# Token rows normed before they are turned, groups loaded one ahead, three bank pairs, recurrence over 17 slots, last projection in 3+3+2 tiles

## The chip, the cores and the metric

One core of one Trainium2 chip. The engines are TensorE (PE, with its weight loads as PEld), VectorE (DVE), ScalarE (ACT), GpSimd (POOL) and SyncE (SP), whose queue issues the DMA transfers here. The metric is the device time of one execution in microseconds (us), the median of several runs.

## What is computed

Two layers over 1040 tokens (16 meta tokens ahead of 1024) of width 1024, float32 throughout; the meta tokens are dropped at the end.

```python
h = concat(meta, x)
# layer 0: pooling mixer
v, gate = split(rmsnorm(h, w0) @ w_in)            # 1024 -> 2 x 2048
u = (trailing mean over 2, 4, 8, 16 tokens) - v   # one window per group of 512 columns
u = einsum(u, w_grp) * scale                      # per group, 512 x 512
h = h + (u * silu(gate)) @ w_out
# layer 1: HGRN2 mixer, 16 heads of 128
q, fp, i, gate = split(rmsnorm(h, w1) @ w_in)     # 1024 -> 4 x 2048
f = lb + (1 - lb) * sigmoid(fp);  k = 1 - f;  q = silu(q)
# per head, chunkwise: S_t = diag(f_t) S_{t-1} + k_t i_t^T ;  o_t = S_t^T q_t
o = rmsnorm(o, per head) * o_norm
h = h + (o * silu(gate)) @ w_out
out = rmsnorm(h[16:], final_w)
```

## The kernel before

**Products.** Activations lie turned: columns of the model on the partitions, tokens along the free dimension, in two passes of 520 tokens, each of 2 x 260 (`CH`). A float32 matmul is made of three: every operand is split into a rounded part and a rest (`split`: a cast on ScalarE, a subtraction on VectorE). The products with `pool_w_in` and `hgrn_w_in` go by a Strassen-like scheme (`products`): two column tiles at a time (v and gate; q and gate; f and i) take seven pieces P1, P2, P6, P5, P7, P3, P4 of 12 matmuls per pass. Two PSUM bank pairs take the sums: P1, P6, P7 and P4 go on in one, P2, P5 and P3 in the other, and in between ScalarE copies them out or VectorE adds them to a copy, so a piece waits for the reader of the piece before it in its pair. The split weights of a piece are made `LOOK = 3` pieces ahead.

**Order.** After each piece `tick()` runs what `later(k, fn)` put there, k pieces on, and then prepares weights. So the other work of a stage is interleaved with the pieces of the next. The framework then orders the instructions of each engine at compile time: a list schedule in which the order of emission is the priority, so a ready instruction of lower priority may stand earlier. On the chip each engine works in that order.

**Stages.** `prologue(p)`: loads five token tiles, turns each (eight transposes by PE, copied out of PSUM), and makes the norm's factor from the rows (Square, `rstd_into` on VectorE and POOL, `rbcast` as matmul L151 to spread it over the partitions); `make_T` then norms the turned halves (L270) and splits all operands of the pieces, in steps s1 to s6. Pass 1's steps run in the ticks of the first tile's pass 0. `v_gate`, `pooled`: 16 column tiles; `u` and the gate go to DRAM. `grp_stage(p)`: per group four `u` tiles are loaded and split and four column tiles multiplied (24 matmuls each, lines 499 to 501). `out_stage(p)`: eight column tiles of 96 matmuls; the residual is loaded in turned form and added on VectorE (L515). `between(p)`: turns the result back to token rows for the norm's factor and for `h_dram`, then `make_T`. Pass 0's steps run in the ticks of `grp_stage(1)`, those of pass 1 in the ticks of head 0's first product.

`mixer1`: 16 heads, each of two products (q and gate, f and i) over both passes. `scan(n)` puts the pieces of head n's recurrence into the ticks of head n+1 (`PIECES`, slots 0 to 12): `run` (a scan and four reciprocals on VectorE, L693), `turn_v`, `scale`, `score`, two levels, `turn_k`, `states`, `outs` (the sums stay in PSUM until they are normed), `gated`. Small sums and transposes use four single banks (`ps_at`).

`out1`: the last projection in four rounds of two token tiles; for each head 12 matmuls of 512 columns (lines 920 to 922). `prep` loads head n's output and gate, multiplies them (L892) and splits them; the last heads' pieces run in the ticks of round 0, what is left by `flush`. After head 15 the residual, the norm and the store follow for both tiles.

Of the kernel before, what the change touches and what calls it, by code (L numbers as in the profile page):

```python
# [40 lines left out]
PIECES = {"run": 0, "turn_v": 1, "scale": 2, "score": 4, "l32": 5, "l64": 6, "turn_k": 7, "states": 8, "outs": 10, "gated": 12}  # L41
# [7 lines left out]
def kernel(  # L49
# [22 lines left out]
    ps_mm = ctx.enter_context(tc.tile_pool(name="ps_mm", bufs=2, space=bass.MemoryType.PSUM))  # L72
    ps_at = ctx.enter_context(tc.tile_pool(name="ps_at", bufs=4, space=bass.MemoryType.PSUM))
# [6 lines left out]
    x_dram = dr.tile([KD, P, L], F32, tag="x", name="x_dram")  # L80
# [68 lines left out]
    def rbcast(dst, rstd, tn):  # L149

        pe.matmul(dst, lhsT=rstd[:tn, 0:1].to_broadcast([tn, P]), rhs=ident[:tn, :tn], start=True, stop=True)  # L151

# [4 lines left out]
    def whole(fast):  # L157
# [8 lines left out]
        def half(name):  # L166
            return un.tile([P, 2, CH], F32, tag="h", name=name, bufs=6)
# [35 lines left out]
        def wslot():  # L203
            return wp.tile([P, 2, 512], F32R, tag="w", name="w", bufs=6)
# [56 lines left out]

        def make_T(p, src, R, w):

            hn, d = [None] * 4, {}

            def norm(i):
                t = unit("hn").rearrange("p (k t) -> p k t", k=2)
                for j in range(2):
                    k = 2 * i + j
                    vec.scalar_tensor_tensor(t[:, j], src[i][:, j], w[:, k : k + 1], R, mul, mul)  # L270
                hn[i] = t.rearrange("p k (c t) -> p k c t", c=2)
# [8 lines left out]
            def B(k, c):  # L280
                return [hn[2 * k + i][:, :, c] for i in range(2)]
# [10 lines left out]
            def s1():  # L292
                norm(0), norm(1)
                put("P1", B(0, 0))

            def s2():
                norm(2), norm(3)
                put("P2", B(1, 0))
# [18 lines left out]
            return [s1, s2, s3, s4, s5, s6]  # L317

# [47 lines left out]

        def token_stats(xt, tn, R, t0):

            ssq, r = small("ssq"), small("rstd", 6)
            act.activation(xt[:tn, :D], xt[:tn, :D], AF.Square, accum_out=ssq[:tn, 0:1])  # L370
            rstd_into(r, ssq, tn, 1, D)
            rb = atbank()
            rbcast(rb[:, :tn], r, tn)
            vec.tensor_copy(R[:, t0 : t0 + tn], rb[:, :tn])

        def load_tokens(p):
            out_ = []
            for t0, tn in TP[p]:
                xt = unit("xt")
                if t0 == 0:  # L380
                    nc.sync.dma_start(xt[:tn, :D], meta_tokens)
                else:
                    nc.sync.dma_start(xt[:tn, :D], x[t0 - META : t0 - META + tn])
                out_.append(xt)
            return out_

        def prologue(p):

            xr = [unit("xr").rearrange("p (k t) -> p k t", k=2) for _ in range(4)]
            R = half("R").rearrange("p a b -> p (a b)")  # L390
            toks = load_tokens(p)

            def turn(i):
                (t0, tn), xt = TP[p][i], toks[i]
                o = t0 - p * PT
                for h in range(2):
                    b = atbank().rearrange("p (k t) -> p k t", t=P)
                    for k in range(4):
                        kk = h * 4 + k
                        pe.transpose(out=b[:, k, :tn], in_=xt[:tn, kk * P : (kk + 1) * P], identity=ident[:tn, :tn])  # L400
                    act.copy(xr[2 * h][:, :, o : o + tn], b[:, 0:2, :tn])
                    vec.tensor_copy(xr[2 * h + 1][:, :, o : o + tn], b[:, 2:4, :tn])
                token_stats(xt, tn, R, o)

            def keep():
                for i in range(4):
                    nc.sync.dma_start(
                        x_dram[2 * i : 2 * i + 2, :, p * PT : (p + 1) * PT].rearrange("k p t -> p k t"), xr[i]
                    )

            steps = make_T(p, xr, R, nw[0])
            return [lambda i=i: turn(i) for i in range(len(TP[p]))] + steps[:2] + [keep] + steps[2:]
# [55 lines left out]

        def grp_stage(p):
            a = {}  # L470
            for g in range(4):
                us, sgs = [], []
                for k in range(4):
                    ur = half("ur").rearrange("p a b -> p (a b)")
                    nc.sync.dma_start(ur, u_dram[g * 4 + k][:, p * PT : (p + 1) * PT])
                    u = unit("u", F32R).rearrange("p (h t) -> p h t", h=2)
                    split(u[:, 0], u[:, 1], ur)
                    us.append(u)
                for j in range(4):
# [9 lines left out]
                    a[m] = at  # L489
                    tick()  # L490
# [12 lines left out]
        def out_stage(p, a):  # L503
            hs = []
            for m in range(KD):
                if m % 2 == 0:
                    h = unit("h").rearrange("p (k t) -> p k t", k=2)
                    nc.sync.dma_start(h, x_dram[m : m + 2, :, p * PT : (p + 1) * PT].rearrange("k p t -> p k t"))
                    hs.append(h)
# [4 lines left out]
                o = hs[-1][:, m % 2].rearrange("p (c t) -> p c t", c=2)  # L514
                vec.tensor_tensor(o, o, ps[:, :, :CH], add)  # L515
            return hs
# [25 lines left out]
        def between(p, hs):  # L542

            R = half("R").rearrange("p a b -> p (a b)")

            def stats(t0, tn):
                ssq, r = small("ssq"), small("rstd", 6)
                ht = unit("ht")
                o = t0 - p * PT
                for h in range(2):  # L550
                    b = atbank()
                    for k in range(4):
                        kk = h * 4 + k
                        pe.transpose(
                            out=b[:tn, k * P : (k + 1) * P], in_=hs[kk // 2][:, kk % 2, o : o + tn], identity=ident
                        )
                    act.copy(ht[:tn, h * 512 : h * 512 + 512], b[:tn])
                    act.activation(b[:tn], b[:tn], AF.Square, accum_out=ssq[:tn, h : h + 1])
                if t0 > 0:
                    nc.sync.dma_start(h_dram[t0 - META : t0 - META + tn], ht[:tn, :D])  # L560
                vec.tensor_tensor(ssq[:tn, 2:3], ssq[:tn, 0:1], ssq[:tn, 1:2], add)
                rstd_into(r, ssq[:, 2:3], tn, 1, D)
                rb = atbank()
# [401 lines left out]
        for fn in prologue(0):  # L965
            fn()
# [57 lines left out]
```

## Time and profile before

| | us |
|---|---|
| median of 3 runs | 1861.88 (1861.18 to 1862.97) |
| profiled execution | 1864.24, its span 1862.5 |
| PE busy | 1718.2 (92%) |
| PEld busy | 1648.1 (88%) |
| VectorE busy | 1256.9 (67%) |
| ScalarE busy | 756.9 (41%) |
[...]

The span runs from the first to the last instruction; 1.74 us of the execution lie around it. Busy shares are means over stages with different limits, and since matmuls are pipelined, busy PE is not PE at its peak.

### The profile page before, as it was taken

Reading aid. Unit: us, or ns where it says so; the run is one execution under the profiler, and the core shown is the slowest. Engines: PE = TensorE matmul, PEld = TensorE weight load, DVE = VectorE, ACT = ScalarE, POOL = GpSimd, SP = SyncE. Lnnn points to the kernel's source line nnn. Section 1 sums busy time; section 2 is a strip of 40 time slices with the busy share of each in tenths; the row PEclk is TensorE's granted clock in tenths of the full one; section 3 lists DMA queues with packets and bytes.
Section 4 is the critical chain, followed back from the end, with each engine's and each line's share of the span. In section 5 each row is a group of like instructions: output and inputs, shape, how many; then the busy total and the mean of one; then the engine's idle time right before and its main releaser. Section 6 shows DMA issues by size and latency. Waiting matters only on the chain.

```text
span 1862.5 us, 32892 instructions
## 1 busy us (share of the span) xinstructions
PE 1718.2 (92%) x13531; PEld 1648.1 (88%) x13531; DVE 1256.9 (67%) x2018; ACT 756.9 (41%) x1696; POOL 49.4 (3%) x70
## 2 busy tenths in 40 slices
PE   4699999998997799699999999999999999988997
PEld 3599999988997699599999999999999999977885
DVE  5766767876425833787778777778877778875432
ACT  4443333344225422535544445444445544444221
POOL 1100000000000000000000000000000000000000
PEclk9899999998998799799999999999999999999999
DMA  4333332356425442211212112112212112245542
GB/s 128 119 109 103 108 111 92 112 177 218 151 91 182 141 127 70 85 58 53 67 47 69 52 57 63 58 58 58 66 50 63 53 58 58 80 158 176 171 142 69
DMA packets 202078, 181.90 MB, mean 98 GB/s; under 512 B 8030, under 2 KB 176046, under 8 KB 201918
## 3 DMA queue, kind: packets, MB, share of 16 engines
q1 hardware_dynamic: 201918, 179.71, 30.6%
q8 instruction: 108, 1.77, 0.4%
q14 instruction: 52, 0.43, 0.1%
HBM read 133.08 MB, written 46.60 MB: 96 GB/s over the span
## 4 chain that ended last, share of the span: by engine, by line
PE 75%; DVE 12%; ACT 6%; issue 4%; POOL 2%; DMA 1%; SPq 0%; DVEq 0%; ACTq 0%; POOLq 0%
PE mm L338 14%; PE mm L340 13%; PE mm L339 13%; PE mm L500 5%; PE mm L499 5%; PE mm L501 5%; DVE F L693 4%; PE at L662 2%; POOL rstd L104 2%; PE at L920 2%; PE at L922 2%; PE at L921 2%; PE at L708 2%; PE at L807 2%; ACT on L834 2%
## 5 line engine op out<-in xcount | busy, mean ns | idle before, releaser
L338 PE MATMUL mm<-Th,w 128*128 128x260 f32 x2688 | 782.3, 291 | 43.2 <-DVE Q L611 23.3
L339 PE MATMUL mm<-Tl,w 128*128 128x260 f32 x2688 | 768.1, 286 | 5.4 <-DVE Tl L147 5.3
L340 PE MATMUL mm<-Th,w 128*128 128x260 f32 x2688 | 768.3, 286 | 0.0
L338 PEld LDWEIGHTS mm<-Th,w 128*128 128x128 f32 x2688 | 513.5, 191 | 52.4 <-DVE Q L611 26.4
L339 PEld LDWEIGHTS mm<-Tl,w 128*128 128x128 f32 x2688 | 513.7, 191 | 8.0 <-DVE Tl L147 7.9
L340 PEld LDWEIGHTS mm<-Th,w 128*128 128x128 f32 x2688 | 513.7, 191 | 0.7
L146 ACT CAST w<-raw 128x512 fp32r<-128x512 f32 x346 | 207.0, 622 | 256.0 <-PE mm L501 193.5
L147 DVE TENSOR_TENSOR w<-raw,w 128x512 fp32r<-128x512 f32 x346 | 232.0, 685 | 117.0 <-ACT w L146 116.4
L344 ACT COPY P<-mm 128x520 f32<-128x520 f32 (+1 forms) x150 | 85.8, 572 | 185.9 <-PE mm L340 185.6
L499 PE MATMUL mm<-a,w 128*128 128x260 f32 x512 | 145.2, 284 | 0.0
L500 PE MATMUL mm<-a,w 128*128 128x260 f32 x512 | 144.3, 282 | 0.0
L501 PE MATMUL mm<-a,w 128*128 128x260 f32 x512 | 143.8, 281 | 0.0
L693 DVE RECIPROCAL F<-X 128x260 f32<-128x260 f32 x64 | 106.9, 1733 | 0.0
L147 DVE TENSOR_TENSOR w<-S,w 128x512 fp32r<-128x512 f32 x100 | 67.5, 686 | 57.1 <-ACT w L146 57.1
L499 PE MATMUL mm<-u,w 128*128 128x260 f32 x256 | 78.4, 311 | 25.2 <-ACT u L146 25.2
L501 PEld LDWEIGHTS mm<-a,w 128*128 128x128 f32 x512 | 96.3, 188 | 0.0
L500 PEld LDWEIGHTS mm<-a,w 128*128 128x128 f32 x512 | 96.3, 188 | 0.0
L499 PEld LDWEIGHTS mm<-a,w 128*128 128x128 f32 x512 | 96.1, 188 | 0.0
L104 POOL TENSOR_TENSOR rstd<-rstd,nhalf 128x1 f32<-128x1 f32 (+4 forms) x44 | 43.3, 984 | 1789.8 <-DVE rstd L103 1150.4
L500 PE MATMUL mm<-u,w 128*128 128x260 f32 x256 | 78.3, 307 | 2.9 <-DVE u L147 2.8
L146 ACT CAST w<-S 128x512 fp32r<-128x512 f32 x100 | 60.9, 627 | 42.7 <-DVE S L236 36.4
L499 PEld LDWEIGHTS mm<-u,w 128*128 128x128 f32 x256 | 53.7, 212 | 26.7 <-ACT u L146 26.4
(160 smaller groups left out, 2605.6 us busy)
## 6 DMA issues: line engine op xcount, KB each, us to landing
raw<-in_hgrn_w_in_dram SPq DMA_DIRECT2D x66, 512.0 KB, 4.2
raw<-in_pool_w_in_dram SPq DMA_DIRECT2D x34, 512.0 KB, 5.3
raw<-in_pool_w_out_dram SPq DMA_DIRECT2D x32, 512.0 KB, 3.6
u_dram<-d SPq DMA_DIRECT2D x16, 520.0 KB, 2.7
ur<-u_dram SPq DMA_DIRECT2D x32, 260.0 KB, 3.7
sgh<-s_dram SPq DMA_DIRECT2D x32, 260.0 KB, 3.7
raw<-in_pool_w_grp_dram SPq DMA_DIRECT2D x16, 512.0 KB, 3.6
a_dram<-og SPq DMA_DIRECT2D x16, 512.0 KB, 2.7
```

The source lines that it names most:

```text
L104: pool.tensor_tensor(r[:tn, :n], r[:tn, :n], nhalf[:tn, :n], ALU.pow)
L146: act.copy(hi, src)
L147: vec.tensor_tensor(lo, src, hi.bitcast(F32), sub)
L338: pe.matmul(o, lhsT=w[:, 0, ks], rhs=th[:, k], start=first, stop=False, **kw)
L339: pe.matmul(o, lhsT=w[:, 0, ks], rhs=tl[:, k], start=False, stop=False, **kw)
L340: pe.matmul(o, lhsT=w[:, 1, ks], rhs=th[:, k], start=False, stop=k == 3, **kw)
L344: act.copy(t[:, s], bs)
L499: pe.matmul(o, lhsT=w[:, 0, ks], rhs=xs[k][:, 0, cs], start=first and k == 0, stop=False)
L500: pe.matmul(o, lhsT=w[:, 0, ks], rhs=xs[k][:, 1, cs], start=False, stop=False)
L501: pe.matmul(o, lhsT=w[:, 1, ks], rhs=xs[k][:, 0, cs], start=False, stop=last and k == 3)
L662: pe.matmul(b[s0 : s0 + h, c * h : (c + 1) * h], lhsT=K0[:, c * P + s0 : c * P + s0 + h], rhs=Q[:, c * P + s0 + h : c * P + s0 + 2 * h], s ...
L693: vec.reciprocal(iX[:, s], X[:, s])
```

## The change

- `tokens(p, w, ys)` takes the place of `prologue` and `between`: per tile, `first` loads the rows of x, adds the result of the layer (turned to rows, VectorE), stores them in `h_dram`, and norms the rows (Square, `rstd_into`, a scaled copy on ScalarE); `second`, two steps later, turns the normed rows and multiplies by the norm's weights on the way out of PSUM. `x_dram`, `rbcast` and the norm in `make_T` go. Before the second layer's pass 0 the steps run in every second tick.
- `group(p, g)` loads and splits the `u` tiles of a group one group ahead; the first of each pass in the stage before.
- `ps_mm` has three pairs in place of two, `ps_at` two banks in place of four; `half` tiles 8 in place of 6, `wslot` 5 in place of 6.
- Head 0's two products run in pass 0 first and then in pass 1.
- The recurrence has 17 slots: the reciprocals and the scores stand alone, `outs` copies its sums out of PSUM, `normed` follows, and `gated` multiplies by the gate (loaded as `gl`), which `prep` did.
- `out1` has rounds of 3, 3 and 2 token tiles; the last three heads of a round are multiplied tile by tile, each tile's end behind its own.

```diff
+PIECES = {
+    "run": 0, "turn_v": 1, "inv0": 1, "inv1": 2, "scale_q": 2, "inv2": 3, "inv3": 4, "scale_k": 5, "scale_e": 6,
+    "score0": 6, "score1": 7, "to32": 8, "l32": 9, "l64": 10, "turn_k": 11, "states": 12, "outs": 14, "normed": 16, "gated": 17,
+}
...
+        def tokens(p, w, ys=None):
+            hn, held = [], {}
+            def first(i):
+                t0, tn = TP[p][i]
+                o = t0 - p * PT
+                ht, sq = unit("ht"), unit("sq")
+                src = meta_tokens if t0 == 0 else x[t0 - META : t0 - META + tn]
+                nc.sync.dma_start(ht[:tn, :D], src)
+                ssq, r = small("ssq", 3), small("rstd", 3)
+                if ys is not None:
...
+                        vec.tensor_tensor(hh, hh, b[:tn], add)
+                    if t0 > 0:
+                        nc.sync.dma_start(h_dram[t0 - META : t0 - META + tn], ht[:tn, :D])
+                act.activation(sq[:tn, :D], ht[:tn, :D], AF.Square, accum_out=ssq[:tn, 0:1])
+                rstd_into(r, ssq, tn, 1, D)
+                act.activation(sq[:tn, :D], ht[:tn, :D], AF.Copy, scale=r[:tn, 0:1])
+                held[i] = sq
+            def second(i):
...
+                    for k in (0, 1):
+                        kk = h * 4 + k
+                        act.activation(hn[2 * h][:, k, o : o + tn], b[:, k, :tn], AF.Copy, scale=w[:, kk : kk + 1])
+                    ww = w[:, h * 4 + 2 : h * 4 + 4].unsqueeze(2).to_broadcast([P, 2, tn])
+                    vec.tensor_tensor(hn[2 * h + 1][:, :, o : o + tn], b[:, 2:4, :tn], ww, mul)
...
+        def group(p, g):
+            us = []
+            for k in range(4):
+                ur = half("ur").rearrange("p a b -> p (a b)")
+                nc.sync.dma_start(ur, u_dram[g * 4 + k][:, p * PT : (p + 1) * PT])
+                u = unit("u", F32R).rearrange("p (h t) -> p h t", h=2)
+                split(u[:, 0], u[:, 1], ur)
+                us.append(u)
+            ready_u[p, g] = us
...
+                    if j == 0 and g < 3:
+                        group(p, g + 1)
...
+                if m == 5 and p == 0:
+                    group(1, 0)
...
-                vec.tensor_tensor(o, o, ps[:, :, :CH], add)
+                act.copy(hs[-1][:, m % 2].rearrange("p (c t) -> p c t", c=2), ps[:, :, :CH])
...
+                    act.copy(ends, X.rearrange("p (b i) -> p b i", i=16)[:, :, 15:16])
+                def inv(i):
+                    s = slice(i * CH, (i + 1) * CH)
+                    vec.reciprocal(iX[:, s], X[:, s])
...
+                    tl["g"] = [half("gl").rearrange("p a b -> p (a b)")[:, :512] for _ in range(2)]
+                    for i, g in enumerate(tl["g"]):
+                        nc.sync.dma_start(g, g_dram[n][:, META + i * 512 : META + i * 512 + 512])
...
+                        act.copy(on[b0 // 4], b)
...
-                        act.activation(og[:, b0 * P : b0 * P + 512], b, AF.Copy, scale=onorm[:, n : n + 1])
+                        vec.scalar_tensor_tensor(og[:, s], b, onorm[:, n : n + 1], tl["g"][b0 // 4], mul, mul)
...
+            puts = [[consumer(part, 0, st) for part in parts] for parts in ("qg", "fi")]
+            for p in range(2):
+                for put in puts:
+                    products((p,), *put)
+                if p == 0:
+                    flush()
...
+            ROUNDS = ((0, 3), (3, 3), (6, 2))
...
-                vec.tensor_tensor(ar, ar, gr, mul)
...
+                for n in range(HEADS - 3):
+                    fetch(r * HEADS + n + 3)
...
+                fetch((r + 1) * HEADS + 2)
+                late = [ready.pop((r, n)) for n in range(HEADS - 3, HEADS)]
...
+                    for j, w in enumerate(late):
+                        proj(ps, w, HEADS - 3 + j, i)
...
-        early(1, 2 * HEADS, lambda t: head_views(t // 2)[t % 2])
+        early(2, 2 * HEADS, view1)
...
+            if t == ME - 1:
+                later(3, lambda: group(0, 0))
...
-        spread(between(0, hs))
+        spread(tokens(0, nw[1], hs), 2)
```

## Rows read from the trace of the kernel before

**Rows 1.** Busy time of each engine by stage; last: granted clock, DMA share, GB/s.

```profile
core 0: us, PE busy (x) PEld busy (x) DVE busy (x) ACT busy (x) POOL busy (x), PEclk, DMA share, GB/s
0.00:36.02 36.02, 12.66 (x54) 10.15 (x54) 14.45 (x41) 13.74 (x29) 4.74 (x27) 1.00 0.55 163
36.02:101.40 65.38, 43.98 (x219) 39.29 (x219) 52.91 (x94) 31.38 (x59) 7.58 (x9) 0.84 0.28 95
101.40:404.63 303.23, 303.23 (x2522) 302.96 (x2520) 217.53 (x327) 107.17 (x220) 0.00 (x0) 1.00 0.34 111
404.63:469.97 65.34, 54.26 (x385) 52.63 (x385) 46.66 (x69) 28.78 (x50) 0.00 (x0) 0.87 0.69 224
469.97:561.97 92.00, 92.00 (x770) 92.00 (x769) 30.45 (x45) 22.58 (x37) 0.00 (x0) 1.00 0.38 118
561.97:647.54 85.57, 61.55 (x437) 59.09 (x436) 59.81 (x100) 43.31 (x83) 3.17 (x5) 0.82 0.51 164
647.54:739.31 91.77, 91.77 (x770) 91.77 (x769) 32.62 (x47) 20.52 (x33) 0.00 (x0) 1.00 0.33 99
739.31:811.91 72.60, 55.32 (x388) 51.42 (x387) 51.45 (x95) 38.99 (x82) 3.16 (x5) 0.84 0.26 81
811.91:1643.55 831.64, 807.09 (x7097) 790.27 (x7095) 642.93 (x991) 389.74 (x960) 24.56 (x15) 1.00 0.20 60
1643.55:1717.37 73.82, 63.15 (x330) 50.58 (x331) 51.60 (x79) 33.20 (x71) 1.64 (x1) 0.93 0.52 172
1717.37:1850.60 133.23, 133.23 (x577) 107.99 (x575) 51.86 (x126) 26.05 (x69) 3.45 (x6) 1.00 0.44 137
1850.60:1862.50 11.90, 0.00 (x1) 0.00 (x0) 4.65 (x10) 1.43 (x6) 1.10 (x2) 0.64 0.25 93
```

**Rows 2.** Waits of PE: us in total, times, longest.

```profile
PE at L151 <- POOL rstd L104: 34.1, 18, 4.2
...
PE mm L499 <- ACT u L146: 25.2, 6, 11.0
...
PE mm L338 <- DVE Q L611: 23.3, 15, 1.7
```

**Rows 3.** Timeline in head 2: VectorE's reciprocals, the add, PE's next product.

```profile
870.73 6.68 DVE L693 RECIPROCAL F<-X 128x260 f32<-128x260 f32 x4
...
877.33 0.64 DVE L611 TENSOR_TENSOR Q<-P,mm 128x520 f32<-128x520 f32 x1
...
878.02 0.39 PE L338 MATMUL mm<-Th,w 128*128 128x260 f32 x1 [1.65 <-DVE Q L611]
```

**Rows 4.** Busy time in the first column tile of `grp_stage(0)`.

```profile
408.21:414.11 5.90, 5.15 (x24) 4.85 (x25) 4.63 (x8) 1.74 (x3) 0.00 (x0) 0.56 0.95 309
```

**Rows 5.** Groups of instructions by line: busy us, mean ns.

```profile
L147 DVE TENSOR_TENSOR w<-raw,w 128x512 fp32r<-128x512 f32 x346 | 232.0, 685 | 117.0 <-ACT w L146 116.4
...
L834 ACT ACTIVATE on<-at,rstd 128x128 f32<-128x128 f32 x128 | 34.8, 383 | 32.8 <-POOL rstd L104 32.8
...
L554 PE MATMUL at<-ident,h 128*128 128x128 f32 (+3 forms) x80 | 12.4, 300 | 0.0
...
L270 DVE SCALAR_TENSOR_TENSOR hn<-xr,vecs,R 128x520 f32<-128x520 f32 x16 | 11.2, 753 | 0.0
...
L370 ACT ACTIVATE xt<-xt 128x1024 f32<-128x1024 f32 (+3 forms) x10 | 10.6, 1059 | 5.3 <-PE at L400 5.3
...
L402 DVE COPY xr<-at 128x256 f32<-128x256 f32 (+3 forms) x20 | 7.3, 373 | 6.6 <-ACT xr L401 6.6
...
L934 DVE TENSOR_TENSOR hres<-hres,at 128x512 f32<-128x512 f32 x8 | 5.2, 683 | 13.8 <-PE at L922 13.7
```

**Rows 6.** Timeline of the projection: after `outs` of head 15, its first matmul, the end.

```profile
1693.89 0.48 PE L920 MATMUL mm<-woh,w 128*128 128x512 f32 x1
...
1712.14 0.80 PE L920 MATMUL mm<-woh,w 128*128 128x512 f32 x1 [4.29 <-ACT w L146]
...
1853.14 1.28 DVE L934 TENSOR_TENSOR hres<-hres,at 128x512 f32<-128x512 f32 x2
```

More of the change, by code (lines that the diff above doesn't have):

```diff
@@ L260, in whole, with make_T @@
         T = {n: [None, None] for n in PRODUCTS}
[L262 to L271, printed above, removed]
+        def make_T(p, hn):
+            d = {}
             def put(name, srcs):
@@ L280, in B @@
             def B(k, c):
-                return [hn[2 * k + i][:, :, c] for i in range(2)]
+                return [hn[2 * k + i].rearrange("p k (c t) -> p k c t", c=2)[:, :, c] for i in range(2)]
             def diff(name, xs, ys):
@@ L365, in cols @@
             return w[:, :, t * P : (t + 1) * P]
[L367 to L412, printed above, removed]
         def make_mask():
@@ L471, in grp_stage @@
             for g in range(4):
[L472 to L478, printed above, removed]
+                us = ready_u.pop((p, g))
                 for j in range(4):
@@ L540, in feed_out @@
                     feed.extend((one, lambda one=one: one(j=1)))
[L542 to L563, printed above, removed]
-                rbcast(rb[:, :tn], r, tn)
-                vec.tensor_copy(R[:, o : o + tn], rb[:, :tn])
-            return [lambda t=t: stats(*t) for t in TP[p]] + make_T(p, hs, R, nw[1])
@@ L713, in score @@
                     vec.tensor_tensor(Fe[:, 24:56], ee[:, :, 0], eo[:, :, 0], mul)
-                return {"run": run, "scale": scale, "score": score}
+                do = {"run": run, "scale_q": scale_q, "scale_k": scale_k, "scale_e": scale_e, "to32": to32}
+                do.update({f"inv{i}": lambda i=i: inv(i) for i in range(4)})
+                do.update({f"score{i}": lambda i=i: score(4 * i) for i in range(2)})
+                return do
             def intra(Q, K, F, Fe):
@@ L841, in gated @@
                         for c in range(4):
-                            pe.transpose(out=b[:, c * P : (c + 1) * P], in_=on[:, b0 + c], identity=ident)
-                        act.activation(og[:, b0 * P : b0 * P + 512], b, AF.Copy, scale=onorm[:, n : n + 1])
+                            pe.transpose(out=b[:, c * P : (c + 1) * P], in_=on[b0 // 4][:, c], identity=ident)
+                        s = slice(b0 * P, b0 * P + 512)
+                        vec.scalar_tensor_tensor(og[:, s], b, onorm[:, n : n + 1], tl["g"][b0 // 4], mul, mul)
                     nc.sync.dma_start(a_dram[n], og)
                 do = {
-                    "turn_v": turn_v, "turn_k": turn_k, "states": states, "outs": outs, "gated": gated,
+                    "turn_v": turn_v, "turn_k": turn_k, "states": states, "outs": outs, "normed": normed, "gated": gated,
                     "l32": lambda: level(Q, K0, 32, Fe[:, 24:56], Fe[:, 0:16]),
@@ L871, in mixer1 @@
+            for n in range(HEADS):
+                if n > 0:
+                    st = {}
+                    for parts in ("qg", "fi"):
+                        products((0, 1), *[consumer(part, n, st) for part in parts])
+                scan(n, st["Q"], st["K"], st["F"], st["ti"])
             out1()
         def out1():
-            NR = SEQ // 256
-            wo, ready = {}, []
-            fnw = []
+            wo, ready = {}, {}
+            ROUNDS = ((0, 3), (3, 3), (6, 2))
+            fnw = unit("fnw")
@@ new lines, in proj @@
+            def proj(ps, w, n, i):
+                wh, wl = wo[n]
+                ts = slice(i * P, (i + 1) * P)
+                for nh in range(2):
+                    s = slice(nh * 512, nh * 512 + 512)
+                    pe.matmul(ps[i][nh], lhsT=w[:, 0, ts], rhs=wh[:, s], start=n == 0, stop=False)
+                    pe.matmul(ps[i][nh], lhsT=w[:, 0, ts], rhs=wl[:, s], start=False, stop=False)
+                    pe.matmul(ps[i][nh], lhsT=w[:, 1, ts], rhs=wh[:, s], start=False, stop=n == HEADS - 1)
@@ L984, in whole @@
         flush()
-        mixer1(between(1, hs))
+        mixer1(tokens(1, nw[1], hs))
         es.close()
```

294 lines of the change are left out of this document (152 added, 142 removed).

## Prediction

> **What bounds the kernel now.** I read first the busy times by stage [rows 1]: the span cut at points that I took from the timeline of PE (first matmul of each kind of work). The reader is to see two sorts of stages there. In 101.40 to 404.63, 469.97 to 561.97 and 647.54 to 739.31 PE is busy without a gap: 768 matmuls of 260 columns in 92.00 us, 0.1198 us each, which is the floor used below. In the others PE is short of work, and its granted clock falls with it (0.82 to 0.87). There I read the waits [rows 2]. At the start of the kernel and at both seams PE waits for a norm (18 waits, 34.1 us, in place L151); at the groups of the pooled stage it waits for the cast of `u` (6 waits, 25.2 us); in the heads it waits once per head for VectorE's add of `Q` (15 waits, 23.3 us). Of that last one there is a case in full [rows 3]: four reciprocals hold VectorE for 6.68 us, the add stands behind them, and the first matmul of product P5 starts 1.65 us late. Nothing else in a head is as long. So PE sets the end in all stages, and what the change can give is PE's gaps, stage by stage; the sum is made so.
>
> A gap costs twice, since the clock is lower after it: the first 24 matmuls of the group stage take 5.90 us at a mean clock of 0.56 [rows 4] against 24 x 0.1198 = 2.88 at full clock, 3.0 us lost.
>
> **The change part by part.**
>
> *Start to tile t=1 (0 to 101.40).* Before, PE's transposes of a token tile stand behind the previous tile's matmul L151, which waits for Square, VectorE and POOL. Now a row is normed before it is turned, and step i turns tile i-2. VectorE loses, over both passes, 16 products (L270, 0.753 each, 12.0 us) and 20 copies (L402, 0.373, 7.5 us), and gets 20 products of 256 columns out of PSUM: between 0.373 and 0.753 (half the width of L270), taken as 0.42, nearer the narrow row: 8.4 us [rows 5]. Its 67.4 us of busy time (14.45 + 52.91) become 56. ScalarE loses its 20 copies of the same width (counted like L402's, 7.5 us) and gets 10 scaled copies of whole rows (at least L370's 1.06, at most that plus L834's 0.383, taken as 1.2) and 40 scaled copies of 128 columns (at most 0.383): 12 + 15.3 - 7.5 = 20 us more, so 65 us in place of 45.1. ScalarE becomes the busiest. The busiest engine was in use for 67.4 / 101.4 = 66% of the stretch; at 66% ScalarE needs 98 us, at 82% 79. The long serial wait goes, so I take 74%: 88 us. The new order also puts each row load at its own step in SP's queue, where before the second pass's five loads stood behind weight loads. A new wait comes in: ScalarE's scaled copy waits for POOL's power, and weight casts are queued behind it; they are made three pieces ahead, which covers it. Term: -13 (-22 to -3).
>
> *Is ScalarE the wrong place?* The rows say VectorE is the fuller engine here, 67.4 against 45.1 us [rows 1]. [...]
>
> *Group stage of pass 0 (404.63 to 469.97).* It takes 65.34 us for 384 matmuls, 46.0 at the floor. The first gap, three later ones and the slow clock are the 19 us between. Now the four `u` tiles of a group are loaded and split a group ahead (16 more instructions moved per group, none added), the first group in the last product tile. What is late next is DMA: 224 GB/s at a share of 0.69 here, 309 at 0.95 in its first tile [rows 1, 4]. 224 x 65.34 = 14.6 MB at 309 / 0.95 = 325 GB/s are 45 us, so the floor of PE and that of DMA meet. I take 52: -13 (-18 to -6).
>
> *Group stage of pass 1 with the seam (561.97 to 647.54).* 85.57 us. PE needs 46.0 and for 5 tiles 16 transposes each; L554's 80 take 12.4 busy us, which overlap, so 54 to 58. VectorE's 59.81: less 8 products (6.0), plus 10 residual adds of 512 columns (L934, 0.683: 6.8) and 10 products of 0.42: 65 if nothing moved. But the steps run every second tick, so that the last five of 13 fall behind the 16 ticks of this stage, into the next, where VectorE is busy 32.62 of 91.77 us and PE has no gap: there they cost nothing, and here VectorE falls under PE. I take 64 us: -22 (-29 to -12).
>
> *Seam to head 0 (739.31 to 811.91).* 72.60 us. The first pass now covers both products, 14 pieces of 12 matmuls, so PE has 20 us of work beside the token steps in place of 10. For this weights of f and i are prepared twice: 7 more splits and 4 sums at 0.685 (L147), 7.5 us of VectorE. Its 51.45 become 51.45 - 6.0 + 6.8 + 4.2 + 7.5 = 64. At the same share (71%) that is 90 us, at 95% 67. VectorE becomes the bound of the seam, and a bound engine runs fuller; I take 88%: 73 us. Term: 0 (-6 to +17).
>
> *Heads (811.91 to 1643.55).* The four reciprocals get four slots behind the add, the banks get a third pair; the wait of 23.3 us goes. It costs 15 scores in two parts and other changes of operation at PE, some 0.1 us each: -21 (-25 to 0). What is late next is the add of the gate after P7, which must be done within one piece (24 x 0.1198 = 2.9 us) before P4 writes that bank; its worst queue is one reciprocal (1.7) and one add. The gate's product moves from the last stage into the head: two more VectorE instructions, at most 0.753 each, 1.5 us per head: 642.93 + 22.6 = 665.5 of 811, 82%. The two loads of `gl` per head go past SP with DMA at a share of 0.20. With two single banks in place of four, the third batch of `turn_v` and `outs` wait for copies; products stand ready to fill that.
>
> *Last projection (1643.55 to 1850.60).* 133.23 us for 577 matmuls, 0.231 each, unchanged. In the first round PE is busy 63.15 of 73.82 us. Head 15's gate output comes 18.25 us after its last score-value matmul (1693.89 to 1712.14), and PE idles 4.29 of that [rows 6]. Now `outs`, `normed` and `gated` of head 15 stand in slots 14 to 17, behind 13 steps of 18 matmuls, and only 36 matmuls of the three tiles (8.3 us) are left to cover these 18.25: some 10 us idle, as much as the whole round has now (73.82 - 63.15). The stall behind the reciprocals in this round goes, this one grows: 0 (-8 to +8).
>
> *End.* From the last matmul to the end 11.90 us. The last tile's add starts 2.54 us late (1853.14 [rows 6]) since the tile before it is finished in the same moment; now that one is finished 18 matmuls sooner: -2.5.
>
> Sum: -13 - 13 - 22 + 0 - 21 + 0 - 2.5 = -71.5. The profiled execution took 1864.24 us, 2.36 over the median of the three runs; 1864.24 - 71.5 - 2.36 = 1790 us in terms of that median, 1861.88.
>
> **Rivals.** *The seams stay bound by VectorE and ScalarE.* Both are the fullest there after the change, and no row shows them above 72% over a seam of this sort. The first terms are then -4, -6, -10 and +8, the whole -35.5: 1826. Against it: their idle time before comes from a chain that the two-step lag opens. Chance 0.13.
>
> *The head's wait only moves* to the add of the gate or to a bank: the change does not do in the heads what it says. The heads' term is 0: 1811. For it speaks VectorE at 82%, against it the 2.9 us of slack. 0.10.
>
> [...] 0.08.
>
> *All seams reach PE's floor*: -22, -18, -31, -13, -25, -8, -2.5: 1742. 0.04.
>
> *Slower: the two single banks.* Each head passes through them in turn_v, scores, levels, turn_k, states, outs, gated. If once per head PE waits for a copy long enough for the clock to fall, the price is the 3.0 us above [rows 4], and the wait, some 2: 5.0 a head, 75 in 15 heads, which takes all of the 71.5. From 71.5 / 15 = 4.8 us a head on it decides. Against it: the stretch of the heads has a clock of 1.00 although each head has a pause of 1.65 us. [...] 0.06, with a third of it near no change.
>
> **How the numbers follow.** My forecast has 0.59. The range of 80% runs from 1760 to 1830: the square root of the summed squares of the half ranges is about 23, the lower end lies a little below 1790 - 23 since some terms have more room downwards, and the upper end is stretched to take in the first three rivals; the last two lie outside. Faster by over 0.2% (about what a measurement of this kernel can tell from none, some 4 us): 0.94; within it: 0.02; slower: 0.04.
>
> **What would show it.** Right: no wait of P5's first matmul for `Q` in the heads, and heads of about 54.1 us in place of 55.5; no PE gap at the groups' first matmuls; t=1 at about 88 us; the seam of pass 1 at about 64; a PE gap of about 10 us at the end of the first projection round, for `ar` of head 15. Wrong: PE waits on single banks in the heads, or a granted clock under 1.00 there; ScalarE over 85% busy before t=1; VectorE under 75% in the seam to head 0 with PE idle, which would mean a chain that I did not see; raw weight loads held up in SP behind `gl` or `ur`.

## The result and the profile after

The changed kernel takes 1796.82 us (median of 4 runs, 1796.19 to 1798.58), the kernel before 1862.43 beside it: a ratio of 0.965, 95% interval 0.9633 to 0.9667. Forecast were 1790, and 1760 to 1830 as range. Spans: 1794.4 against 1862.5 us, at a mean granted TensorE clock of 0.981 against 0.970.

Busy time by stage of the changed kernel, the answer to [rows 1]:

```profile
core 0: us, PE busy (x) PEld busy (x) DVE busy (x) ACT busy (x) POOL busy (x), PEclk, DMA share, GB/s
0.00:36.02 36.02, 9.67 (x44) 7.41 (x44) 11.36 (x31) 20.35 (x41) 4.37 (x27) 1.00 0.35 104
36.02:98.86 62.84, 40.97 (x211) 35.97 (x209) 43.48 (x76) 40.02 (x78) 9.85 (x9) 0.73 0.23 72
...
404.27:449.31 45.04, 45.01 (x376) 44.79 (x375) 42.59 (x66) 26.02 (x47) 0.00 (x0) 1.00 0.90 298
...
541.15:604.93 63.78, 58.47 (x466) 56.06 (x465) 45.52 (x81) 39.69 (x79) 3.59 (x5) 0.97 0.69 216
...
697.03:776.97 79.94, 61.24 (x422) 55.62 (x420) 57.99 (x107) 47.78 (x101) 3.19 (x5) 0.87 0.35 108
776.97:1575.26 798.29, 797.87 (x7055) 784.78 (x7054) 661.45 (x1018) 404.98 (x969) 22.92 (x14) 1.00 0.23 72
1575.26:1671.27 96.01, 88.23 (x466) 71.89 (x465) 52.99 (x74) 40.18 (x97) 3.51 (x2) 0.96 0.43 142
1671.27:1784.73 113.46, 111.78 (x481) 89.88 (x480) 31.98 (x68) 20.92 (x54) 3.86 (x7) 1.00 0.27 88
1784.73:1794.40 9.67, 0.00 (x0) 0.00 (x0) 3.36 (x7) 1.33 (x4) 0.55 (x1) 0.75 0.31 114
```

| stage | before, us | after, us | forecast | measured |
|---|---|---|---|---|
| start to t=1 | 101.40 | 98.86 | -13 (-22 to -3) | -2.5 |
| other pool products and group stage of pass 0 | 368.57 | 350.45 | -13 (-18 to -6) | -18.1 |
| group stage of pass 1 with the seam | 85.57 | 63.78 | -22 (-29 to -12) | -21.8 |
| seam to head 0 | 72.60 | 79.94 | 0 (-6 to +17) | +7.3 |
| heads | 831.64 | 798.29 | -21 (-25 to 0) | -33.3 |
| last projection | 207.05 | 209.47 | 0 (-8 to +8) | +2.4 |
| end | 11.90 | 9.67 | -2.5 | -2.2 |

The second row is measured from t=1 to the first matmul of `out_stage(0)`, since the scheduler now lays the first group's matmuls among the last products. The two `out_stage`s together differ by 0.2. Some 4.4 us of the heads' gain is only moved: `outs` and `gated` of the head before the last now lie in the projection (32 matmuls and 8 transposes, 0.11 us each; at the other end the first of the 15 stretches is shorter, 49.4 us against 53.5). So the heads gave 28.9.

What PE still waits for, over the whole span (us in total, times, longest), against [rows 2]:

```profile
PE at L346 <- ACT sq L333: 19.2, 4, 8.8
PE at L346 <- DVE hn L351: 11.9, 8, 5.6
...
PE mm L922 <- ACT w L148: 3.6, 1, 3.6
```

L346 turns the normed rows; L922 is the projection, waiting for head 15. Of the waits for `u` one of 0.5 us is left, of those for `Q` one of 1.3 us in the seam to head 0; in the heads there is none. VectorE in a head, against [rows 3]: the four reciprocals still end with two in a row ahead of the add of `Q`, and no matmul waits behind it.

```profile
878.62 2.32 DVE L659 TENSOR_TENSOR_SCAN X<-F,Zt 128x1040 f32<-128x1040 f32 x1
...
881.10 1.77 DVE L664 RECIPROCAL F<-X 128x260 f32<-128x260 f32 x1
...
883.81 1.77 DVE L664 RECIPROCAL F<-X 128x260 f32<-128x260 f32 x1
...
887.17 3.40 DVE L664 RECIPROCAL F<-X 128x260 f32<-128x260 f32 x2
...
890.51 0.68 DVE L571 TENSOR_TENSOR Q<-P,mm 128x520 f32<-128x520 f32 x1
```

The scan ends at 880.94, so the add is done 10.3 us after it (891.19). Before it was 7.7 us, from the end of this scan (870.23) to 877.97 [rows 3]:

```profile
867.91 2.32 DVE L690 TENSOR_TENSOR_SCAN X<-F,Zt 128x1040 f32<-128x1040 f32 x1
```

So the add has not become earlier; what has changed is what PE has to do meanwhile. The 32 matmuls of `outs` of the head before, which stand in slot 14 now, lie in this stretch; the first and the last of their rows:

```profile
882.73 0.38 PE L808 MATMUL at<-V,A 128*128 128x128 f32 x2
...
886.08 0.39 PE L809 MATMUL at<-S,Q 128*128 128x128 f32 x2
```

And where one of the two misses sits, the seam to head 0: SP's queue, then the last of VectorE's residual adds.

```profile
713.35 0.32 SPq L330 DMA_DIRECT2D h_dram<-ht  x1
713.72 0.42 SPq L317 DMA_DIRECT2D ht<-in_x_dram  x1
...
721.91 0.34 SPq L330 DMA_DIRECT2D h_dram<-ht  x1
722.31 0.42 SPq L317 DMA_DIRECT2D ht<-in_x_dram  x1
...
729.48 0.33 SPq L330 DMA_DIRECT2D h_dram<-ht  x1
```
```profile
728.17 1.28 DVE L328 TENSOR_TENSOR ht<-ht,at 128x512 f32<-128x512 f32 x2 [1.96 <-DMA ht<-in_x_dram]
```

Each load of a row tile is issued right behind the store of an earlier one, and that store waits for the add of its own tile. Add, store, load, add: the last four adds start 7.0, 8.6 and 7.6 us apart, while VectorE is busy 57.99 of 79.94 us (73%).

### The profile page after: what moved, and what is told of

It is laid out like the page before. It is cut to its first block, busy times and chain, and to the rows that moved or that the text cites. A ratio compares the mean times of both kernels' runs of the same rounds, so it can differ in the third digit from the quotient of the medians.

```text
span 1794.4 us, 32938 instructions
## 1 busy us (share of the span) xinstructions
PE 1701.6 (95%) x13571; PEld 1634.3 (91%) x13571; DVE 1238.1 (69%) x1948; ACT 807.7 (45%) x1783; POOL 51.8 (3%) x70
## 4 chain that ended last, share of the span: by engine, by line
PE 86%; DVE 6%; DMA 3%; ACT 3%; issue 1%; POOL 1%; SPq 0%; DVEq 0%; POOLq 0%; ACTq 0%
PE mm L383 17%; PE mm L385 17%; PE mm L384 17%; PE mm L505 5%; PE mm L506 5%; PE mm L507 5%; PE mm L922 3%; PE mm L924 3%; PE mm L923 3%; PE at L630 2%; DMA ht<-in_x_dram 2%; PE at L683 2%; PE at L787 2%; PE at L809 2%; PE at L808 2%
## 5 line engine op out<-in xcount | busy, mean ns | idle before, releaser
L148 ACT CAST w<-raw 128x512 fp32r<-128x512 f32 x351 | 212.8, 620 | 166.2 <-PE mm L507 106.4
L664 DVE RECIPROCAL F<-X 128x260 f32<-128x260 f32 x64 | 111.3, 1758 | 0.0
L922 PE MATMUL mm<-woh,w 128*128 128x512 f32 x256 | 103.7, 405 | 5.3 <-ACT w L148 3.6
L924 PE MATMUL mm<-woh,w 128*128 128x512 f32 x256 | 102.2, 400 | 0.0
L923 PE MATMUL mm<-wol,w 128*128 128x512 f32 x256 | 102.0, 398 | 0.0
L505 PE MATMUL mm<-u,w 128*128 128x260 f32 x256 | 73.9, 289 | 0.5 <-ACT u L148 0.5
```

The source lines that it names most:

```text
L148: act.copy(hi, src)
L505: pe.matmul(o, lhsT=w[:, 0, ks], rhs=xs[k][:, 0, cs], start=first and k == 0, stop=False)
L664: vec.reciprocal(iX[:, s], X[:, s])
L922: pe.matmul(ps[i][nh], lhsT=w[:, 0, ts], rhs=wh[:, s], start=n == 0, stop=False)
L923: pe.matmul(ps[i][nh], lhsT=w[:, 0, ts], rhs=wl[:, s], start=False, stop=False)
L924: pe.matmul(ps[i][nh], lhsT=w[:, 1, ts], rhs=wh[:, s], start=False, stop=n == HEADS - 1)
```

## The experiments

Times are medians of five runs; the ratio is to the kernel before on the same chip. "A head" is the time from head n's first product matmul to head n+1's, for the heads in the middle.

**Row loads ahead.**

```diff
-            hn, held = [], {}
+            hn, held, hts = [], {}, []
+            for t0, tn in TP[p]:
+                ht = unit("ht")
...
+                nc.sync.dma_start(ht[:tn, :D], src)
+                hts.append(ht)
...
-                nc.sync.dma_start(ht[:tn, :D], src)
...
-        for fn in tokens(0, nw[0]):
+        steps0, steps1 = tokens(0, nw[0]), tokens(1, nw[0])
```

> The five row loads of each turn of the token rows are issued ahead of the turn's first step, so that no store of a finished row tile and no weight load stands before them in SP's queue. Theory (the order of SP's queue binds both places where the changed kernel missed the forecast): the stretch from head 0's first product to head 1's falls from 79.94 us to about 70, the stretch from the first product to t = 1 falls from 62.84 us to about 55, and the time from 1796.8 to about 1779. Rival one (work of VectorE and ScalarE binds both): each stretch stays within 1.5 us and the time within 3 us of 1796.8. Rival two (only one of the two is bound by the queue): the seam alone gives about 1787, the start alone about 1789.

1779.84 us, ratio 0.9556 (0.9543 to 0.9569): 17.0 below the change. Busy time by stage, both seams:

```profile
541.44:597.15 55.71, 55.42 (x466) 54.50 (x465) 47.79 (x84) 41.39 (x81) 3.12 (x5) 1.00 0.68 211
689.05:759.94 70.89, 58.66 (x421) 54.76 (x420) 57.56 (x107) 46.30 (x99) 2.93 (x5) 0.90 0.32 97
```

The same work of VectorE (57.56 against 57.99) now fits in 70.89 us, so it was not the bound; the chain through SP's queue was. The seam of pass 1, which I had not named, had a like chain (there loads of weights and of the gate stand in the queue between store and load as well): 63.78 to 55.71, where PE is left with 0.3 us of gaps. The start gave only 2.4 of the 8 expected: from the first product to t=1 it is 4.4 us shorter (58.48), but the first product comes 2.0 us later (38.03), for a reason in this row of VectorE:

```profile
25.32 0.69 DVE L233 TENSOR_TENSOR S<-raw 128x512 f32<-128x512 f32 x1 [12.73 <-DMA raw<-in_pool_w_in_dram]
```

Ten row tiles now stand ahead of the weights in SP's queue. The compile-time order has this weight sum before the norm's factor, and VectorE stands behind it for 12.73 us.

**Head 0's f and i over both passes again.**

```diff
-            for p in range(2):
-                for put in puts:
-                    products((p,), *put)
-                if p == 0:
-                    flush()
+            products((0,), *puts[0])
+            flush()
+            products((1,), *puts[0])
+            products((0, 1), *puts[1])
```

> Head 0 goes back to the order of before: q and g over pass 0, then over pass 1, then f and i over both passes at once (7 weight splits fewer). Theory (the longer seam to head 0 comes from the chain of stores and loads in SP's queue, not from the order of head 0's products): the seam has less work of TensorE to lay over the row tiles, so it gets longer than 79.94 us, by up to the 26 us of products that no longer lie ahead, if the chain of five row tiles stands alone; with 5 us the time is 1802. Rival (the seven extra splits and the new order cost the 7 us): the stretch goes back to about 72.6 us and the time to about 1789.

1793.66 us, ratio 0.9631 (0.9618 to 0.9644). The seam falls to 75.03 us, so it did not get longer: the extra splits and the order cost 4.9 us, two thirds of what the rival said. (The first stretch, which the edit does not touch, was 3.6 us longer here; why stays open.) The seam's growth thus has two parts, and the first experiment's part is the larger.

**Reciprocals in one slot; two bank pairs; the slots of before.** Four kernels on the heads. First all four reciprocals in slot 2:

> The four reciprocals stand in one slot again, behind each other on VectorE; all else of the recurrence keeps its slots, and the three bank pairs stay. Theory (spreading the reciprocals took away the wait of P5 for Q): the wait of 1.65 us comes back in each of 15 heads, heads go from 53.5 to about 55.1 us, and the time to about 1821. Rival (the third bank pair lets TensorE run on over the block of reciprocals, or the other slots made the room): no gap returns, heads stay at 53.5 us, the time within 4 us of 1796.8.

1801.71 us, ratio 0.9671 (0.9658 to 0.9684); a head takes 53.60 against 53.48, and the seam 1.7 us more. The theory falls in this form: four slots for the reciprocals are worth 0.12 us a head. Then two pairs and four single banks, with the third projection tile in single banks:

> Two bank pairs and four single banks as in the kernel before; the third token tile of a projection round adds up in two single banks. Theory (the slots, not the banks, gave the heads their time): heads stay at 53.5 us, the group stages and the rest too, time within 4 us of 1796.8. Rival (the third pair gave the part of the heads' gain that was not forecast, 0.5 us a head): heads go to about 54.0 us and the time to about 1805. Rival two (two single banks hold TensorE up in the recurrence, which four would end): heads get shorter, under 53.3 us.

1789.98 us, ratio 0.9607 (0.9594 to 0.962); a head 53.48. The third pair gives the heads nothing; from t=1 to `out_stage(0)` it is worth 1.9 us (352.35 against 350.45), and four single banks take 2.3 us off the seam to head 0 and 2.9 off that of pass 1. The whole is 6.8 us shorter though no head is, which none of the three had. Then all slots as before:

```diff
-    "run": 0, "turn_v": 1, "inv0": 1, "inv1": 2, "scale_q": 2, "inv2": 3, "inv3": 4, "scale_k": 5, "scale_e": 6,
-    "score0": 6, "score1": 7, "to32": 8, "l32": 9, "l64": 10, "turn_k": 11, "states": 12, "outs": 14, "normed": 16, "gated": 17,
+    "run": 0, "inv0": 0, "inv1": 0, "inv2": 0, "inv3": 0, "turn_v": 1, "scale_q": 2, "scale_k": 2, "scale_e": 2,
+    "score0": 4, "score1": 4, "to32": 4, "l32": 5, "l64": 6, "turn_k": 7, "states": 8, "outs": 10, "normed": 10, "gated": 12,
```

> The recurrence stands in the slots of the kernel before (scan and all four reciprocals in slot 0, the multiplications in slot 2, both score halves in slot 4, and so on to gated in slot 12); the three bank pairs and all else stay. After the two runs in which neither the reciprocals in one later slot nor two bank pairs gave a head more than 0.12 us, three theories are left. One (either of the two suffices: spread slots, or a third pair that lets TensorE run over the block): heads stay under 53.8 us here, and only with two pairs as well do they go to 55.1 or more; time about 1800. Two (slot 0 is what counts, right behind the scan, where the block stands ahead of the next head's Q): heads 55.1 us here too, time about 1821. Three (neither; the shorter outs, whose banks are copied out at once, gave the gain): heads 53.5 us here and with two pairs.

> As the run with the slots of the kernel before, and two bank pairs with four single banks as well; of the change to the heads only the copied outs, the gate multiplied in at the end of a head and the eight half tiles stay. Theory one (spread slots or a third pair, either suffices): heads 55.1 us or more, that is 1.6 us over the changed kernel, time about 1816 with the 7 us that two pairs gave back elsewhere. Theory two (slot 0 alone): the same here. Theory three (outs gave the gain): heads 53.5 us, time about 1790.

1826.94 us, ratio 0.9806 (0.9793 to 0.982), and with two pairs 1819.57, ratio 0.9757 (0.974 to 0.9774). A head takes 55.86 and 55.85: near theory two's number, but not by its way. In the heads in the middle PE waits for `Q` in neither run, so that slot 0 of the reciprocals counts is not shown; the slots as a whole count, 2.4 us a head, and the pairs do not. The loss has other places. PE's waits over two heads, with three pairs:

```profile
PE at L630 <- DVE K L689: 2.0, 2, 1.0
```
```profile
1000.43 0.14 PEld L829 LDWEIGHTS at<-ident,on 128*128 128x128 f32 x1 [0.16 <-ACT on L821]
1000.73 0.14 PEld L829 LDWEIGHTS at<-ident,on 128*128 128x128 f32 x1 [0.15 <-ACT on L821]
```

The score waits for `K` (1.0 a head), and the transposes of `gated` follow the scaling on ScalarE at 0.3 us each instead of 0.11 (the second view, the timeline of PE's weight loads), some 1.5 us more for eight. In return the last projection is 13.6 us shorter: round 0 takes 83.82 us in place of 96.17 (from its first matmul, which lies 0.16 us ahead of the cut in the table above), since head 15 is done sooner.

**The kernel before with the new slots alone.** Only the pieces of the recurrence are cut and placed as in the change; `outs` keeps its sums in two single banks until they are normed.

> The kernel before, with one part of the change alone: the recurrence cut into the pieces of the changed kernel and put into its slots (one reciprocal a slot, gated in slot 17). Two bank pairs, the old token stage, the old group stage and the old last projection stay. Theory (the slots alone take the head's wait away): a head goes from 55.50 to about 53.6 us, which takes some 28 us from 14 heads; the end of the recurrence of head 15 comes later in the last projection, which gives back up to 10 us there; time about 1842. Rival (slots help only with the third pair or the copied outs): heads stay over 55 us and the time within 8 us of 1862.

1899.01 us, ratio 1.0191 (1.0177 to 1.0205): 1.9% slower than before, and neither theory had that. A head takes 58.05. From the timeline of one head:

```profile
1043.51 2.32 DVE L693 TENSOR_TENSOR_SCAN X<-F,Zt 128x1040 f32<-128x1040 f32 x1
...
1043.75 3.51 POOL L107 TENSOR_TENSOR rstd<-rstd,nhalf 128x8 f32<-128x8 f32 x1 [54.54 <-DVE rstd L106]
...
1047.29 2.17 ACT L846 ACTIVATE on<-at,rstd 128x128 f32<-128x128 f32 x8 [3.97 <-POOL rstd L107]
...
1048.49 0.38 PE L789 MATMUL at<-ident,ti 128*16 128x128 f32 x1 [3.07 <-ACT on L846]
1048.52 0.56 PE L341 MATMUL mm<-Th,w 128*128 128x260 f32 x1
1048.88 0.42 PE L342 MATMUL mm<-Tl,w 128*128 128x260 f32 x1
1049.10 0.42 PE L343 MATMUL mm<-Th,w 128*128 128x260 f32 x1
```

`outs`, now in slot 14, meets `turn_v` of the next head in slot 1. Two single banks are held for the norm's factor, `turn_v` needs three, and PE stands 3.07 us. After it matmuls of 260 columns start 0.22 us apart instead of 0.12 for a while; the granted clock over two heads is 0.97.

**The changed kernel (two pairs) with held `outs`.**

```diff
-                        act.copy(on[b0 // 4], b)
...
-                            act.activation(sq, on[b0 // 4][:, c], AF.Square, accum_out=ssq[:, cc : cc + 1])
+                            act.activation(sq, b[:, c], AF.Square, accum_out=ssq[:, cc : cc + 1])
...
+                        act.activation(on[cc // 4][:, cc % 4], obs[cc // 4][:, cc % 4], AF.Copy, scale=r[:, cc : cc + 1])
```

> The changed kernel with two bank pairs and four single banks (1789.98 us, heads 53.48 us), and one thing more put back: outs leaves its sums in two of the four single banks, squares them there, waits for the row factor and scales them out of the banks in the same slot; no copy at once, no slot of its own for the scaling. Theory (the copied outs are the condition under which spread slots help: held banks make the first transposes of the next head wait, as they did for 3.07 us in each head of the kernel before with the new slots): a gap of about 3 us at the third bank of turn_v in each head, heads 56.5 to 58.1 us, time 1835 to 1860. Rival (that gap belonged to the rest of the kernel before, the wait of GpSimd's power beside VectorE's scan above all): heads stay under 54.0 us, time within 8 us of 1790.

1813.61 us, ratio 0.9736 (0.9723 to 0.9749); a head 55.33, under the forecast 56.5 to 58.1. The gap is there in each head, but smaller:

```profile
995.06 1.64 POOL L106 TENSOR_TENSOR rstd<-rstd,nhalf 128x8 f32<-128x8 f32 x1 [53.71 <-DVE rstd L105]
...
996.73 2.17 ACT L818 ACTIVATE on<-at,rstd 128x128 f32<-128x128 f32 x8 [2.57 <-POOL rstd L106]
...
997.92 0.28 PE L757 MATMUL at<-ident,ti 128*16 128x128 f32 x1 [1.67 <-ACT on L818]
```

GpSimd's power takes 1.64 us here and 3.51 there, where it falls beside the scan. So both theories hold a part: the held banks make the wait; where the power falls beside the scan it is longer by 1.40 us, and so is ScalarE's wait for the power (3.97 against 2.57). The granted clock over two heads is 1.00 here and 0.97 there, with the longer wait. The two kernels differ in more than this, so the second half is read from the rows and not tested alone.

**Groups at their own time.** `group(p, g)` moves back to the head of its group.

> The changed kernel with the pooled groups loaded and split at their own time, as before, not one ahead. Theory (loading ahead is what took the waits from the group stages): each first group of a stage stands 5.9 us again and the later ones some 2 us; the two group stages together are 15 to 25 us longer, the time 1812 to 1822. Rival (the stages gained by the token steps and the third bank pair, and the loads are hidden either way): both stages within 3 us, time 1797 to 1800.

1829.69 us, ratio 0.9818 (0.9803 to 0.9833): 32.9 over the change, more than expected. PE's waits in both stages:

```profile
PE mm L504 <- ACT u L148: 14.2, 6, 3.7
```

From t=1 to the first matmul of `out_stage(0)` it takes 365.45 us (+15.0), and the seam of pass 1 77.83 (+14.1). So loading ahead is 15.0 of the 18.1 us gained in pass 0, and 14.1 of the 21.8 in pass 1.

**Early loads put together with the other parts.**

> Early row loads, two bank pairs with four single banks, and in the first stretch the order five row tiles of pass 0, the two weight tiles of the first pair, five row tiles of pass 1 in SP's queue. Theory (the gains of early loads, 17.0 us, and of four single banks, 6.8 us, lie in different waits): the time is about 1773, with the seam to head 0 under 70 us, and the two weight tiles land at about 17 us instead of 23.5, so that the first product comes at about 33 us instead of 38.0. Rival (the four single banks only eased the same chain of stores and loads): the time stays at about 1779 but for the start.

> As the run before, and head 0's products in the order q and g over pass 0, q and g over pass 1, f and i over both passes. Theory (with the chain of stores and loads gone the seven extra weight splits only cost VectorE, and it bounds the seam): the seam gets about 4 us shorter than with the order of the change, time about 1769. Rival (with loads early the 14 products of pass 0 are what TensorE has to do while the row tiles are turned): the seam gets longer, by 5 us or more.

1780.7 us, ratio 0.9555 (0.9542 to 0.9569), and joined 1776.82, ratio 0.9535 (0.9522 to 0.9548). Here the rival won: with early loads the four single banks save 1.2 us in the seam to head 0 (69.65) and 1.0 in that of pass 1 (54.68). They had eased the same chain. Joined passes give 2.8 us in the seam (66.89). The start got worse: the first product at 42.20 us and, joined, at 42.27 (t=1 at 99.18 and 100.05), with the weight sum as first thing on VectorE again, its tile landing at 20.56 and not at 17. Next the weights go first, and the last head gets shorter slots:

```diff
+        ensure(1)
+        steps0, steps1 = tokens(0, nw[0]), tokens(1, nw[0])
...
-                        later(k, do[name])
+                        later(k * 2 // 3 if n == HEADS - 1 else k, do[name])
```

> The two first weight tiles, then all ten row tiles ahead in SP's queue; two bank pairs with four single banks; head 0 with f and i over both passes at once; and the slots of the last head alone cut to two thirds, so that its gated lies before the last three rows of products of round 0. Theory: against the run with early loads, two pairs and joined passes (1776.8 us) the first product comes 6 to 10 us sooner, as VectorE no longer stands behind the weight tile (t = 1 at about 92), and round 0 loses 6 of its gaps (4.0 and 2.2 us): time about 1764. Rival one (the first stretch is set by VectorE's work after the first product): t = 1 stays at 97 to 100, time about 1771. Rival two (cut slots bring head 15's waits into round 0): round 0 gets no shorter.

1754.39 us, ratio 0.9418 (0.9406 to 0.9431): 42 us under the change, better than either theory. The weight sum, and the stages that moved:

```profile
13.70 0.69 DVE L233 TENSOR_TENSOR S<-raw 128x512 f32<-128x512 f32 x1 [7.59 <-DMA raw<-in_pool_w_in_dram]
```
```profile
536.10:590.79 54.69, 54.69 (x467) 54.34 (x465) 47.63 (x84) 41.51 (x81) 3.12 (x5) 1.00 0.69 214
682.58:748.32 65.74, 56.68 (x419) 53.92 (x418) 53.61 (x97) 43.69 (x88) 2.92 (x5) 0.90 0.30 90
1546.33:1630.58 84.25, 84.25 (x468) 69.94 (x466) 54.89 (x79) 40.25 (x102) 3.83 (x3) 1.00 0.53 174
```

The sum is at 13.70 us, the first product at 35.33, t=1 at 92.03. Round 0 has no gap left: 84.25 us, where the joined run before it has 96.76. Against that run, t=1 comes 8.0 us sooner and round 0 is 12.5 us shorter, which is nearly the whole gain of 22.4.

## Why the prediction was right, and where it was not

The sum was near (-68.1 in the span against -71.5), and part of that is luck. Two gains were forecast too large (start, seam to head 0) and two too small (group stage of pass 0, heads); errors of some 21 us one way and some 17 the other nearly cancel. The terms of the start and of the heads lie outside their own ranges, that of pass 0's group stage just outside.

*Start: the step that failed.* "The long serial wait goes, so I take 74%" did not come true: the wait only changed its place. PE's waits for rows and their norm up to t=1, before (0 to 101.40) and after (0 to 98.86):

```profile
PE at L151 <- POOL rstd L104: 19.2, 9, 3.5
...
PE at L400 <- DMA xt<-in_meta_tokens_dram: 3.9, 1, 3.9
...
PE at L400 <- DMA xt<-in_x_dram: 1.7, 1, 1.7
```
```profile
PE at L346 <- ACT sq L333: 19.2, 4, 8.8
...
PE at L346 <- DVE hn L351: 9.3, 5, 5.6
```

That is 24.8 us before and 28.5 now, for the scaled copy and for the tile before. By the stages, PE idles 48.2 us up to t=1 against 44.8; the stretch is 2.5 us shorter only since PE is busy 6.0 us less. The busy times were right (ScalarE 60.4 us against 65 forecast, VectorE 54.8 against 56; the row copy 1.15 us, taken as 1.2; the product 0.42). The share of 74% was not: the fullest engine was in use for 60.4 / 98.86 = 61%, less than before.

"The new order also puts each row load at its own step in SP's queue" did not come true either: the five loads of pass 1 stand behind weight loads again, at 43.21 us. That queue is a part of the loss: between the joined run and the last one, whose starts differ in nothing but the order of loads in it, t=1 moves from 100.05 (five row tiles, two weight tiles, five row tiles) to 92.03 (the two weight tiles first).

Whether ScalarE was the wrong place stays open. A first stretch with no gain at all, taken at 0.08, would have been nearer the measured -2.5 than my -13. By the shares of busy time neither engine is full (ScalarE 61%, VectorE 55%), but the 19.2 us above end with ScalarE's scaled copy, and no run here tried the other place.

*Group stages.* Right in kind, and pass 1 in size (-21.8 against -22). Pass 0 reached the floor that I had worked out (45.04 us at a DMA share of 0.90 for 376 of its 384 matmuls, forecast 52): a group ahead hides all of it. In pass 1 some 8 us more were to be had, hidden by a chain like that of the next seam.

*Seam to head 0.* The "chain that I did not see", with VectorE under 75%, was there, as the list of signs had it. I had no row for it since the kernel before loads no rows in its seams: the load came into a queue in which a store already waited. Of the 7.3 us lost, early loads give back 9.1 and joined passes 4.9 when made alone; with loads early (and two pairs) joined passes give 2.8.

*Heads.* A head takes 53.48 us, not 54.1: the wait went, and the counter items that I had charged at PE don't show (PE is busy 107.00 us over two heads, 107.49 before; the 0.1 us a change was my estimate: at 873.27 us of the kernel before, the first product behind transposes has 0.20 us to the next start, the others 0.12). But the reason as I put it, four slots for the reciprocals and a third pair, is not what the runs showed: one block of reciprocals costs 0.12 us a head, two pairs nothing. What the timelines show in its place are the 32 matmuls of `outs` between the scan and the add of `Q`; no run moved these alone, so that stays a reading. What the runs do show is that the new slots as a whole and the copied sums need each other. Four corners, us a head:

| | slots 0 to 12 | slots 0 to 17 |
|---|---|---|
| sums held in PSUM | 55.50 (before) | 55.33 (changed kernel), 58.05 (kernel before) |
| sums copied at once | 55.86 | 53.48 |

The changed kernel with held sums and the old slots was not run, so the kernel before stands in that corner. Against its 55.50, either part alone gives at most 0.2 us or costs up to 2.6; together they give 2.0. The rival of the slower side, a wait on a single bank long enough for the clock to fall, priced at 5.0 us a head, did come, at 4.6 against a head without a wait (58.05 - 53.48), in the kernel where the slots were spread without the copy: 3.07 of wait, where I had some 2, and about 1.3 of slower matmuls (PE busy 109.91 against 107.28 us over two heads with the shorter wait), where I had 3.0. In the change the copy of `outs` keeps it out, not the products "ready to fill that". Over two heads the granted clock was 0.97 with pauses of 3.07 us and 1.00 with those of 1.67 us.

*Last projection.* The gap behind head 15 came as forecast: 7.8 us idle in round 0 (96.01 - 88.23), some 10 forecast. PE around it, against [rows 6]:

```profile
1656.38 0.62 PE L829 MATMUL at<-ident,on 128*128 128x128 f32 x2 [1.80 <-ACT on L821]
...
1665.30 0.50 PE L922 MATMUL mm<-woh,w 128*128 128x512 f32 x1 [3.65 <-ACT w L148]
```

Shorter slots for the last head took it away. The end was right to 0.3 us.

What stays open: what sets the first 92 us after the loads are in order (an early first product alone does not: with two pairs and nothing else changed it comes at 32.36 us, and t=1 still at 99.07), and the 3.6 us of the first stretch in the second experiment.

## What to carry to other kernels

Here a load issued behind a store in SP's queue inherited all that the store waited for (adds 7.0 to 8.6 us apart, and 17.0 us less with the loads ahead); look at what stands ahead of each load in its queue, and issue loads ahead of the loop that stores. A gain that needs two parts can show as nothing, or as a loss, when one is tried alone (0.2 us a head at most, or 2.6 lost, against 2.0 for both), so try all four corners before a part is credited. Both terms here that rested on a guessed share of busy time (start, seam to head 0) missed, by 10.5 and 7.3 us: ask first which chain would let the engine be that busy. And a stage whose time comes out right may still hide a wait: pass 1 met its forecast to 0.2 us with 8 us of queue in it.

## What the runs showed of the hardware that was not expected

GpSimd's power of 128 x 8 numbers took 1.65 us on average in the 15 heads of the changed kernel and 3.55 in the 15 of the kernel before with the new slots. In the timeline above it starts 0.24 us after the start of VectorE's scan, which ends at 1045.83; the power ends at 1047.26, 1.43 us later. Beside the scan its row is longer, and shows that as length, not as waiting. (Spans of GpSimd in these profiles are rough.) What makes it longer no run here shows. Work of VectorE beside the power does not always go with a longer one: in the changed kernel VectorE starts a subtraction 0.43 us into it, and neither is longer than elsewhere (1.64 us against 1.65 in the mean, 0.68 against 0.69).

```profile
890.68 1.64 POOL L106 TENSOR_TENSOR rstd<-rstd,nhalf 128x8 f32<-128x8 f32 x1 [51.83 <-DVE rstd L105]
...
891.11 0.68 DVE L149 TENSOR_TENSOR w<-raw,w 128x512 fp32r<-128x512 f32 x1
```
